# A hybrid encoder trunk on one core: S5 turns' tables, a norm's squares, and the gates' place in the scans

## The chip, the core and the metric

The kernel runs on one core of one Trainium2 chip. The metric is the device time of one execution in microseconds (us), median of three runs. Engines by the profile's names: PE is TensorE, PEld its weight loads, DVE is VectorE, ACT is ScalarE, POOL is GpSimd, SP is SyncE, which issues most DMAs.

## The reference, cut to what matters

Two layers on a sequence of 512 tokens with 1024 channels, in float32. Each layer is: RMS norm, one input projection, two mixers side by side, one output projection, residual add, RMS norm, an MLP with squared ReLU, residual add. Layer 0 mixes with RWKV-7 and Mamba-2, layer 1 with S5 (a diagonal complex state space) and mLSTM. The change is in what leads from layer 0's MLP into layer 1's mixers.

```python
def rmsnorm(x, w):
    y = x * rsqrt(mean(x * x, axis=-1) + EPS)
    return y * w

# S5, per direction: state x[t] = abar * x[t-1] + bbar @ u[t], abar = exp(dt * (ar + i*ai))
mag = exp(dt * ar)
abr, abi = mag * cos(dt * ai), mag * sin(dt * ai)

# mLSTM gates, per head and direction, chunkwise with a running maximum
log_i = i_pre + i_b
log_f = log_sigmoid(f_pre + f_b)
b = cumsum(log_f); m_t = max(max(b[t] - b[s] + log_i[s]), b + m)
```

## The kernel before, in words

**Layout.** Activations lie as eight tiles of 128 channels by 512 tokens. A product with a 128-column block of weights is a group of 24 matmuls of 512 columns: the weights are loaded in float32 (`wraw`), split into a high part on ACT (`whi`, L87) and a rest on DVE (`wlo`, L88; on POOL for eight columns of the mLSTM), and each of eight k-blocks takes three matmuls (L99 to L101 in `mm3`, L112 to L114 in `project`). `wraw`, `whi` and `wlo` have two buffers each, and the matmuls of these groups write to two PSUM banks (`mm`).

**Order.** A planner writes each engine's order at build time: it takes instructions by their order in the program as they become ready on its own clock, and the chip then runs each engine's list in that order. In stretches marked as scheduled by hand (layer 1 up to the heads) PE keeps the order of the program; the other engines are still the planner's. A pool's tile may be written when the tiles that lay at its place before have been read for the last time.

**Layer 0's MLP (`mlp`).** Four quarters of up and down groups: an up group's result goes through ACT (`hid`, L219; `act`, L221), POOL (L223) and DVE (L224); a down group's result is evacuated by DVE (`evac`, L251, two buffers) and added to the residual tile `x` by POOL (L253). In program order the groups are 10 up, 8 down, 8 up, 8 down, 8 up, 8 down, 6 up, 8 down. After each group `beside` takes one step of a generator, here `S5.params`, and lets that step's DVE instructions come no earlier than the group's own evacuation.

**The S5 tables (`S5.params`).** 61 steps. Steps 13 to 44 make the matrices of eight blocks of channel groups; steps 45 to 47 write them through DMAs on POOL's queue (L1544, L1547), beside down groups 2 to 4 of the third quarter. Step 48 makes the decay table `rc` (one ACT copy of 2048 columns, L1554, two POOL memsets) and starts the turns, unit complex numbers `z[i]`: `square` takes three DVE instructions and ends with `unit`, four more, which brings the length back to one. Steps 48 to 52 hold eight squares. Steps 53 to 60 double the tables `cos` and `sin` by complex products (`cmul`, six DVE instructions, scratch in the free half of `sin`); the four of the last doubling stand beside down groups 0 to 3 of the last quarter. Step 61 copies the negated sine (one ACT copy of 2048 columns, L1601).

**Layer 1's norm.** `split` makes high and low parts of the eight residual tiles (ACT L128, DVE L129). `rms_scale` squares them on ACT (L140), three buffers; POOL adds them up (L145), six adds; two matmuls with ones sum over channels (L148, L149); ACT takes the root (L160) and DVE the reciprocal `rstd` (L167). The pool `pre1` of these tiles (12 KB a partition) lies on the left side of memory, where the MLP's tiles lay before. The first two column groups of the projection need no `rstd` to start; the third needs a bank, which the first gives back only through L1608, with `rstd`.

**The scans.** `S5.scan` has 20 steps, five for each quarter of the channel groups: two with 16 small matmuls each (L1638) into two banks and three DVE instructions (L1640 to L1642), two with a pair of scans (L1645, L1647), one with the way back (L1650 to L1655). After each step PE gets four dense steps (12 matmuls of the projection). `Mlstm.gates` is a generator of 14 steps; the first two run before the scans. Of the other twelve, call them g3 to g14: g3 is a softplus on DVE, g4 a transpose on PE (L1132) and two cumulative sums, g5 to g8 running maxima, g9 four results of which the first is `li` (L1164), g10 to g13 each a transpose on PE (L1174), of `li` in g11, g14 four small DVE products (`diag`, L1180) and a matmul that sums them (L1182). `S5_STEPS[3]` says from which scan step on one gates step is taken after each scan step: 4, so that g14 follows scan step 15. `S5_STEPS[4]` is the number of dense steps behind each gates step that is left over after the scans; there is none before. Then seven dense steps, the outputs of S5 (L1680 to L1682) with the rest of the 128 dense steps, and the heads.

Of the kernel before, what the change touches and what calls it, by code (L numbers as in the profile page):

```python
# [13 lines left out]
AF = mybir.ActivationFunctionType  # L14
ALU = mybir.AluOpType
# [11 lines left out]
class Core:  # L27
# [102 lines left out]
                                           op0=ALU.mult, op1=ALU.subtract)  # L130
        return hi, lo

    def mean_square(self, xs):

        nc = self.nc
        n = xs[0].shape[1]
        acc = None
        for x in xs:
            sq = self.tile(self.io, [128, n], "sq", 3)
            nc.scalar.activation(sq, x, AF.Square)  # L140
            if acc is None:
                acc = sq
            elif x is not xs[-1]:
                nxt = self.tile(self.io, [128, n], "sqa", 2)
                nc.gpsimd.tensor_tensor(out=nxt, in0=acc, in1=sq, op=ALU.add)  # L145
                acc = nxt
        ps = self.aux()[:, 0:n]
        nc.tensor.matmul(ps, lhsT=self.ones, rhs=acc, start=True, stop=False)  # L148
        nc.tensor.matmul(ps, lhsT=self.ones, rhs=sq, start=False, stop=True)  # L149
        return ps  # L150

    def rms_scale(self, xs, pool, root=True, pieces=False):

        nc = self.nc
        ps = self.mean_square(xs)
        n = xs[0].shape[1]
        t = self.tile(self.io, [128, n], "ms", 1)
        r = self.tile(pool, [128, n], "rstd", 1)
        if root:
            nc.scalar.activation(t, ps, AF.Sqrt, bias=self.eps, scale=1.0 / 1024)  # L160
        else:
            nc.vector.tensor_scalar(out=t, in0=ps, scalar1=1.0 / 1024, scalar2=EPS,
                                    op0=ALU.mult, op1=ALU.add)
        if pieces:
            inverse(nc, r, t)
        else:
            nc.vector.reciprocal(out=r, in_=t)  # L167
        return r
# [98 lines left out]
PREP = (2, 3)  # L267
SPLIT = 6
END = (4, 24)
S5_STEPS = 8, 8, 4, 4, 3  # L270
OUT_STEPS = (0,) * 10 + (0, 1, 1) * 11 + (0,) * 8
NA = 2
DECAY = float(np.exp(-0.5))
# [1055 lines left out]
class S5:  # L1329
# [16 lines left out]
    def params(self, kp, tp):  # L1346

        c, nc = self.c, self.c.nc
# [5 lines left out]
        lent = [x.rearrange("p g c -> p (g c)") for x in (self.cos, self.sin[:, 0], self.sin[:, 1])]  # L1354
# [54 lines left out]
        x = tt(t("x"), dt, ar, M)  # L1409
# [35 lines left out]
        ts(pr[:, 1], am1, 1.0, Ad)  # L1445
        tt(pi[:, 1], mag, sin, M)

        def cmul(outr, outi, ar_, ai_, br_, bi_, shape, eng2=None):

            e2 = eng2 or V  # L1450
            self.n += 1
            names = ("a", "b", "c", "d")[:len(shape) - 1]
            cut = lambda x: x.rearrange(f"p ({' '.join(names)}) -> p {' '.join(names)}", **dict(zip(names, shape[1:])))
            t1, t2, t3, t4 = (cut(lent[2][:, 512 * i:512 * i + int(np.prod(shape[1:]))]) for i in range(4))
            V.tensor_tensor(out=t1, in0=ar_, in1=br_, op=M)
            e2.tensor_tensor(out=t2, in0=ai_, in1=bi_, op=M)
            V.tensor_tensor(out=outr, in0=t1, in1=t2, op=Sb)
            e2.tensor_tensor(out=t3, in0=ar_, in1=bi_, op=M)
            V.tensor_tensor(out=t4, in0=ai_, in1=br_, op=M)
            e2.tensor_tensor(out=outi, in0=t3, in1=t4, op=Ad)  # L1460
# [40 lines left out]
        for gb in range(8):  # L1501
            G = slice(4 * gb, 4 * gb + 4)
# [48 lines left out]
        r8 = tt(t("r8"), mag, mag, M)  # L1551
        tt(r8, r8, r8, M)
        tt(r8, r8, r8, M)
        nc.scalar.activation(self.rc, r8.unsqueeze(2).to_broadcast([128, 32, 64]), AF.Copy)  # L1554
        nc.gpsimd.memset(self.rc[0:64, :, 0:1], 0.0)
        nc.gpsimd.memset(self.rc[64:128, :, 63:64], 0.0)

# [9 lines left out]
        def unit(x):  # L1567
            tt(zq, x, x, M)
            tt(zq[:, 0], zq[:, 0], zq[:, 1], Ad)
            ts(zq[:, 0], zq[:, 0], -0.5, M, 1.5, Ad)  # L1570
            tt(x, x, zq[:, 0:1].to_broadcast([128, 2, 32]), M)

        def square(o, x, two=2.0):
            tt(zq, x, x, M)
            stt(o[:, 1], x[:, 0], two, x[:, 1], M, M)
            tt(o[:, 0], zq[:, 0], zq[:, 1], Sb)
            unit(o)

        unit(z[0])
        square(z[6], z[0])  # L1580
        yield
        square(z[0], z[6])
        square(z[1], z[0], sgn)
        yield
        for i in range(1, 6):
            square(z[i + 1], z[i])
            if i % 2:
                yield

        tr, ti = self.cos, self.sin[:, 0]  # L1590
# [2 lines left out]
        for i in range(6):  # L1593
            k = 1 << i
            n = min(32, 256 // k)
            for G in (slice(g, g + n) for g in range(0, 32, n)):
                b = lambda x: z[i + 1][:, x, G].unsqueeze(2).to_broadcast([128, n, k])
                cmul(tr[:, G, k:2 * k], ti[:, G, k:2 * k], tr[:, G, 0:k], ti[:, G, 0:k], b(0), b(1), (128, n, k))
                if k >= 4:
                    yield  # L1600
        nc.scalar.activation(self.sin[:, 1], ti, AF.Copy, scale=-1.0)  # L1601
        yield

    def columns(self, i, ps, rstd):
        c, nc = self.c, self.c.nc
# [151 lines left out]
def trunk(tc, ap, out):  # L1757
    nc = tc.nc
    with ExitStack() as ctx:
# [130 lines left out]
        with ExitStack() as left:  # L1890
# [8 lines left out]
            w_in = ap["cd_in"]  # L1899
            with ExitStack() as right:  # L1900
                xnp = right.enter_context(pool("xn1", "right"))
                with pool("pre1") as pre:
                    c.io = pre
                    xn = [c.split(x, xnp, 8, mix_w[1][:, k:k + 1]) for k, x in enumerate(X)]
                    rstd = c.rms_scale(X, io)
                c.io = io
                sa = right.enter_context(pool("s5_a", "right"))
                column = lambda i, use, eng=None: c.project(w_in[i], 128, xn, lambda ps: use(ps, rstd), eng)
# [107 lines left out]
```

## Time and profile before

| | us |
|---|---|
| three runs | 1800.29, 1802.35, 1804.42 |
| median | 1802.35 |
| the profiled execution | 1804.32 |
| its span, first to last instruction | 1802.5 |
| PE busy in it | 1697.4 |
| DVE, ACT, POOL busy | 1184.7, 733.7, 543.7 |

The profiled execution lies 1.97 us above the median, and its span 1.8 us below its own time. A row of the waits says which engine stood still, at which line, until which instruction ended. A row of the timeline gives start, duration, engine, line, operation, output and inputs, and in brackets how long the engine was idle before it. A row of busy time by stretch gives the stretch, its length, the busy time of each engine with its count of instructions, the granted TensorE clock as a share of 2.4 GHz, and the share and rate of the DMA engines.

### The profile page before, as it was taken

To read this page: it belongs to the slowest core of one execution; us is meant where nothing else is said; L and a number is where in the kernel's file an instruction comes from. 1 tells how busy PE (TensorE), PEld (TensorE's weight loads), DVE (VectorE), ACT (ScalarE), POOL (GpSimd) and SP (SyncE) were. 2 spreads that over 40 slices of the span, in tenths; PEclk is the share of its full clock that TensorE was granted. 3 is DMA by queue.
4 is the path that set the end of the run, shared out by engine and by line. 5 is a ranking of instruction groups with operands and counts; after the bars stand their busy time and mean duration, and the time that the engine had idled before them with its cause. 6 is when DMAs were issued, how large, how long until landed. Compare 5 with 4: busy or idle time off the path is not lost.

```text
span 1802.5 us, 26376 instructions
## 1 busy us (share of the span) xinstructions
PE 1697.4 (94%) x10124; PEld 1355.1 (75%) x10124; DVE 1184.7 (66%) x2110; ACT 733.7 (41%) x1263; POOL 543.7 (30%) x528
## 2 busy tenths in 40 slices
PE   7989999999899999999998989799799999999997
PEld 5777767678677877777786767587577688888887
DVE  6879796876777386657465849964658734353545
ACT  5635454433743343231322333335746432323243
POOL 4312131310452214666551323300221222222222
PEclk9999999899899999999998999889999999999999
DMA  4230202123402222433351366354321333323241
GB/s 166 80 94 19 66 25 80 29 71 117 143 13 80 75 93 75 136 101 122 129 173 60 101 204 167 122 184 108 89 87 53 100 93 94 94 94 105 94 132 67
DMA packets 90046, 177.40 MB, mean 98 GB/s; under 512 B 32688, under 2 KB 39600, under 8 KB 89792
## 3 DMA queue, kind: packets, MB, share of 16 engines
q1 hardware_dynamic: 82176, 157.32, 28.4%
q0 software_dynamic: 3200, 11.05, 1.8%
q10 hardware_dynamic: 4544, 7.34, 1.1%
q8 instruction: 80, 1.31, 0.3%
q14 instruction: 46, 0.38, 0.1%
HBM read 149.24 MB, written 28.54 MB: 99 GB/s over the span
## 4 chain that ended last, share of the span: by engine, by line
PE 38%; DVE 8%; ACT 3%; issue 3%; POOL 2%; DMA 0%; DVEq 0%; POOLq 0%; ACTq 0%
PE mm L99 10%; PE mm L100 9%; PE mm L101 9%; PE mm L112 1%; PE mm L113 1%; PE mm L114 1%; DVE wlo L88 1%; DVE s_w L1647 1%; PE mm L1272 1%; POOL hid L223 1%; POOL sqa L145 0%; DVE s_w L1642 0%; ACT whi L87 0%; DVE s_w L1645 0%; PE mm L1277 0%
## 5 line engine op out<-in xcount | busy, mean ns | idle before, releaser
L99 PE MATMUL mm<-act,whi 128*128 128x512 f32 (+1 forms) x1264 | 486.6, 386 | 12.1 <-ACT hid L219 3.1
L101 PE MATMUL mm<-act,wlo 128*128 128x512 f32 (+1 forms) x1264 | 483.9, 383 | 5.4 <-DVE wlo L88 5.0
L100 PE MATMUL mm<-act,whi 128*128 128x512 f32 (+1 forms) x1264 | 482.6, 382 | 0.6 <-DVE act L126 0.5
L87 ACT ACTIVATE whi<-wraw 128x1024 fp32r<-128x1024 f32 (+1 forms) x230 | 227.4, 989 | 581.2 <-PE mm L100 450.3
L88 DVE TENSOR_TENSOR wlo<-wraw,whi 128x1024 fp32r<-128x1024 f32 (+1 forms) x222 | 300.4, 1353 | 176.1 <-ACT whi L87 173.4
L99 PEld LDWEIGHTS mm<-act,whi 128*128 128x128 f32 x1264 | 239.2, 190 | 62.1 <-ACT hid L219 4.4
L101 PEld LDWEIGHTS mm<-act,wlo 128*128 128x128 f32 x1264 | 239.5, 190 | 56.8 <-DVE wlo L88 11.5
L100 PEld LDWEIGHTS mm<-act,whi 128*128 128x128 f32 x1264 | 239.7, 190 | 48.0 <-DVE act L126 1.4
L112 PE MATMUL mm<-act,whi 128*128 128x512 f32 (+1 forms) x464 | 205.3, 442 | 2.2 <-DVE pad L77 1.8
L114 PE MATMUL mm<-act,wlo 128*128 128x512 f32 (+1 forms) x464 | 188.2, 406 | 2.2 <-DVE wlo L88 2.2
L113 PE MATMUL mm<-act,whi 128*128 128x512 f32 (+1 forms) x464 | 186.7, 402 | 0.0
L223 POOL TENSOR_TENSOR hid<-hid 128x512 f32<-128x512 f32 x64 | 94.4, 1475 | 237.5 <-ACT hid L219 228.3
L253 POOL TENSOR_TENSOR x<-x,evac 128x512 f32<-128x512 f32 x56 | 83.8, 1497 | 184.0 <-DVE evac L251 176.1
L251 DVE TENSOR_TENSOR evac<-mm,rstd 128x512 f32<-128x512 f32 (+1 forms) x72 | 45.2, 628 | 108.0 <-PE mm L101 108.0
L112 PEld LDWEIGHTS mm<-act,whi 128*128 128x128 f32 (+1 forms) x464 | 89.4, 193 | 27.4 <-issue 4.5
L114 PEld LDWEIGHTS mm<-act,wlo 128*128 128x128 f32 (+1 forms) x464 | 89.3, 192 | 25.2 <-DVE wlo L88 3.1
L113 PEld LDWEIGHTS mm<-act,whi 128*128 128x128 f32 (+1 forms) x464 | 89.7, 193 | 15.6 <-issue 1.7
L224 DVE TENSOR_TENSOR act<-hid,act 128x512 fp32r<-128x512 f32 x64 | 45.0, 704 | 60.1 <-POOL hid L223 60.1
L145 POOL TENSOR_TENSOR sqa<-sqa,sq 128x512 f32<-128x512 f32 (+1 forms) x30 | 38.4, 1279 | 45.3 <-ACT sq L140 43.3
L76 POOL MEMSET pad<- 128x2 f32 x34 | 3.6, 111 | 152.8 <-DVE sh L768 55.3
L77 DVE TENSOR_TENSOR pad<-mm,rstd 128x512 f32<-128x512 f32 x32 | 21.9, 684 | 42.3 <-PE mm L114 42.3
L1753 DVE TENSOR_TENSOR x<-mm,x 128x512 f32<-128x512 f32 x32 | 22.1, 690 | 40.9 <-PE mm L101 40.9
(562 smaller groups left out, 2858.9 us busy)
## 6 DMA issues: line engine op xcount, KB each, us to landing
wraw<-mlp_w SPq DMA_DIRECT2D x130, 512.0 KB, 3.5
wraw<-ab_in SPq DMA_DIRECT2D x34, 512.0 KB, 3.7
wraw<-cd_in SPq DMA_DIRECT2D x21, 512.0 KB, 3.6
x<-x SPq DMA_DIRECT2D x16, 256.0 KB, 4.0
wraw<-ab_out_b SPq DMA_DIRECT2D x8, 512.0 KB, 3.6
s_cm<-s_sin POOLq DMA_DIRECT2D x8, 512.0 KB, 4.7
s_bm<-s_bt POOLq DMA_DIRECT2D x8, 512.0 KB, 4.6
s_m<-s_bm SPq DMA_DIRECT2D x8, 512.0 KB, 6.0
```

The lines of the kernel that those rows point to most:

```text
L87: nc.scalar.activation(hi[:, :cols], raw[:, :cols], AF.Copy)
L88: (eng or nc.vector).tensor_tensor(out=lo[:, :cols], in0=raw[:, :cols], in1=hi[:, :cols].bitcast(F32), op=ALU.subtract)
L99: nc.tensor.matmul(out, lhsT=wh, rhs=xh, start=start and k == 0, stop=False)
L100: nc.tensor.matmul(out, lhsT=wh, rhs=xl, start=False, stop=False)
L101: nc.tensor.matmul(out, lhsT=wl, rhs=xh, start=False, stop=stop and k == n - 1)
L112: nc.tensor.matmul(out, lhsT=wh, rhs=xh, start=k == 0, stop=False)
L113: nc.tensor.matmul(out, lhsT=wh, rhs=xl, start=False, stop=False)
L114: nc.tensor.matmul(out, lhsT=wl, rhs=xh, start=False, stop=k == len(xs) - 1)
L223: nc.gpsimd.tensor_tensor(out=sq, in0=h, in1=h, op=ALU.mult)
L224: last[0] = nc.vector.tensor_tensor(out=lo, in0=sq, in1=hi.bitcast(F32), op=ALU.subtract)
L251: last[0] = nc.vector.tensor_tensor(out=t, in0=ps, in1=r2[:, a:b], op=ALU.mult)
L253: (nc.vector if b - a < T else nc.gpsimd).tensor_tensor(out=x, in0=x, in1=t, op=ALU.add)
```

## The change

Three edits. `S5.params` writes `rc` in two copies with a step each, normalises only `z[0]` and `z[1]` instead of all nine turns, goes through the last doubling from the highest groups down with its scratch in 1024 instead of 2048 columns, and copies the negated sine in three pieces as groups are done; it still has 61 steps, and each of the doublings' steps stands one group later than before. Layer 1's norm squares into the tile that later holds the mean (`ms`) and one more, 4 KB instead of 12, and its pool moves to the right side, above the tiles of `split`. The gates start after scan step 11 instead of 4, so that g12 to g14 are left over and take three dense steps each behind them.

```diff
--- before.py
+++ after.py
@@ -130,11 +130,21 @@
                                            op0=ALU.mult, op1=ALU.subtract)
         return hi, lo
 
-    def mean_square(self, xs):
+    def mean_square(self, xs, lean=None):
 
         nc = self.nc
         n = xs[0].shape[1]
         acc = None
+        if lean is not None:
+            acc, last = lean, self.tile(self.io, [128, n], "sq", 1)
+            for i, x in enumerate(xs):
+                nc.scalar.activation(last if i else acc, x, AF.Square)
+                if 0 < i < len(xs) - 1:
+                    nc.gpsimd.tensor_tensor(out=acc, in0=acc, in1=last, op=ALU.add)
+            ps = self.aux()[:, 0:n]
+            nc.tensor.matmul(ps, lhsT=self.ones, rhs=acc, start=True, stop=False)
+            nc.tensor.matmul(ps, lhsT=self.ones, rhs=last, start=False, stop=True)
+            return ps
         for x in xs:
             sq = self.tile(self.io, [128, n], "sq", 3)
             nc.scalar.activation(sq, x, AF.Square)
@@ -149,12 +159,12 @@
         nc.tensor.matmul(ps, lhsT=self.ones, rhs=sq, start=False, stop=True)
         return ps
 
-    def rms_scale(self, xs, pool, root=True, pieces=False):
+    def rms_scale(self, xs, pool, root=True, pieces=False, lean=False):
 
         nc = self.nc
-        ps = self.mean_square(xs)
         n = xs[0].shape[1]
         t = self.tile(self.io, [128, n], "ms", 1)
+        ps = self.mean_square(xs, t if lean else None)
         r = self.tile(pool, [128, n], "rstd", 1)
         if root:
             nc.scalar.activation(t, ps, AF.Sqrt, bias=self.eps, scale=1.0 / 1024)
@@ -267,7 +277,7 @@
 PREP = (2, 3)
 SPLIT = 6
 END = (4, 24)
-S5_STEPS = 8, 8, 4, 4, 3
+S5_STEPS = 8, 8, 4, 11, 3
 OUT_STEPS = (0,) * 10 + (0, 1, 1) * 11 + (0,) * 8
 NA = 2
 DECAY = float(np.exp(-0.5))
@@ -1445,13 +1455,14 @@
         ts(pr[:, 1], am1, 1.0, Ad)
         tt(pi[:, 1], mag, sin, M)
 
-        def cmul(outr, outi, ar_, ai_, br_, bi_, shape, eng2=None):
+        def cmul(outr, outi, ar_, ai_, br_, bi_, shape, eng2=None, room=512):
 
             e2 = eng2 or V
             self.n += 1
             names = ("a", "b", "c", "d")[:len(shape) - 1]
             cut = lambda x: x.rearrange(f"p ({' '.join(names)}) -> p {' '.join(names)}", **dict(zip(names, shape[1:])))
-            t1, t2, t3, t4 = (cut(lent[2][:, 512 * i:512 * i + int(np.prod(shape[1:]))]) for i in range(4))
+            n = int(np.prod(shape[1:]))
+            t1, t2, t3, t4 = (cut(lent[2][:, room * i:room * i + n]) for i in range(4))
             V.tensor_tensor(out=t1, in0=ar_, in1=br_, op=M)
             e2.tensor_tensor(out=t2, in0=ai_, in1=bi_, op=M)
             V.tensor_tensor(out=outr, in0=t1, in1=t2, op=Sb)
@@ -1551,7 +1562,9 @@
         r8 = tt(t("r8"), mag, mag, M)
         tt(r8, r8, r8, M)
         tt(r8, r8, r8, M)
-        nc.scalar.activation(self.rc, r8.unsqueeze(2).to_broadcast([128, 32, 64]), AF.Copy)
+        for G in (slice(0, 16), slice(16, 32)):
+            nc.scalar.activation(self.rc[:, G], r8[:, G].unsqueeze(2).to_broadcast([128, 16, 64]), AF.Copy)
+            yield
         nc.gpsimd.memset(self.rc[0:64, :, 0:1], 0.0)
         nc.gpsimd.memset(self.rc[64:128, :, 63:64], 0.0)
 
@@ -1574,17 +1587,17 @@
             tt(zq, x, x, M)
             stt(o[:, 1], x[:, 0], two, x[:, 1], M, M)
             tt(o[:, 0], zq[:, 0], zq[:, 1], Sb)
-            unit(o)
 
         unit(z[0])
         square(z[6], z[0])
         yield
         square(z[0], z[6])
         square(z[1], z[0], sgn)
+        unit(z[1])
         yield
         for i in range(1, 6):
             square(z[i + 1], z[i])
-            if i % 2:
+            if i in (3, 5):
                 yield
 
         tr, ti = self.cos, self.sin[:, 0]
@@ -1593,13 +1606,16 @@
         for i in range(6):
             k = 1 << i
             n = min(32, 256 // k)
-            for G in (slice(g, g + n) for g in range(0, 32, n)):
+            for g in range(32 - n, -1, -n):
+                G = slice(g, g + n)
                 b = lambda x: z[i + 1][:, x, G].unsqueeze(2).to_broadcast([128, n, k])
-                cmul(tr[:, G, k:2 * k], ti[:, G, k:2 * k], tr[:, G, 0:k], ti[:, G, 0:k], b(0), b(1), (128, n, k))
+                cmul(tr[:, G, k:2 * k], ti[:, G, k:2 * k], tr[:, G, 0:k], ti[:, G, 0:k], b(0), b(1), (128, n, k), room=256)
+
+                G = G if g else slice(0, 16)
+                if k == 32 and g != 8:
+                    nc.scalar.activation(self.sin[:, 1, G], ti[:, G], AF.Copy, scale=-1.0)
                 if k >= 4:
                     yield
-        nc.scalar.activation(self.sin[:, 1], ti, AF.Copy, scale=-1.0)
-        yield
 
     def columns(self, i, ps, rstd):
         c, nc = self.c, self.c.nc
@@ -1899,10 +1915,10 @@
             w_in = ap["cd_in"]
             with ExitStack() as right:
                 xnp = right.enter_context(pool("xn1", "right"))
-                with pool("pre1") as pre:
+                with pool("pre1", "right") as pre:
                     c.io = pre
                     xn = [c.split(x, xnp, 8, mix_w[1][:, k:k + 1]) for k, x in enumerate(X)]
-                    rstd = c.rms_scale(X, io)
+                    rstd = c.rms_scale(X, io, lean=True)
                 c.io = io
                 sa = right.enter_context(pool("s5_a", "right"))
                 column = lambda i, use, eng=None: c.project(w_in[i], 128, xn, lambda ps: use(ps, rstd), eng)
```

## Rows read from the trace of the kernel before

**Rows 1.** waits of PE, 930 to 1200: total us, times, longest us

```profile
PE aux L1174 <- DVE ml_li L1164: 10.6, 1, 10.6
PE aux L148 <- POOL sqa L145: 5.3, 1, 5.3
PE mm L99 <- DVE s_zq L1376: 2.9, 1, 2.9
PE mm L99 <- ACT hid L219: 2.8, 2, 1.4
PE mm L99 <- DVE evac L251: 2.8, 1, 2.8
PE aux L1182 <- DVE ml_diag L1180: 2.4, 1, 2.4
```

**Rows 2.** busy time by stretch: length, engines, clock, DMA share, GB/s

```profile
950.00:960.00 10.00, 7.08 (x19) 5.33 (x18) 5.45 (x16) 1.06 (x1) 1.28 (x1) 0.66 0.24 84
...
980.00:990.00 10.00, 10.00 (x39) 8.06 (x38) 9.88 (x40) 2.18 (x3) 4.64 (x5) 0.83 0.14 50
...
1005.00:1045.00 40.00, 39.99 (x176) 32.73 (x176) 32.66 (x49) 14.07 (x17) 14.80 (x12) 1.00 0.34 107
```

**Rows 3.** timeline of DVE, 951 to 979

```profile
951.98 1.23 DVE L88 TENSOR_TENSOR wlo<-wraw,whi 128x1024 fp32r<-128x1024 f32 x1 [4.15 <-ACT whi L87]
953.12 0.69 DVE L251 TENSOR_TENSOR evac<-mm,rstd 128x512 f32<-128x512 f32 x1
...
978.83 0.68 DVE L251 TENSOR_TENSOR evac<-mm,rstd 128x512 f32<-128x512 f32 x1
```

**Rows 4.** groups of DVE instructions, 940 to 1026: busy us, mean ns of one

```profile
L1376 DVE TENSOR_TENSOR s_zq<-s_zq 128x32 f32<-128x32 f32 x9 | 2.5, 278 | 0.2
L1368 DVE TENSOR_SCALAR s_zq<-s_zq 128x32 f32<-128x32 f32 x9 | 2.5, 273 | 0.2
L1376 DVE TENSOR_TENSOR s_z<-s_z,s_zq 128x64 f32<-128x64 f32 x9 | 2.0, 223 | 0.2
```

**Rows 5.** timeline of ACT, POOL, PE and DVE at the norm

```profile
1042.54 0.40 PE L112 MATMUL mm<-act,whi 128*128 128x512 f32 x1
...
1044.84 0.72 ACT L128 ACTIVATE act<-x,c_norms 128x512 fp32r<-128x512 f32 x1 [1.27 <-POOL pad L76]
1045.47 1.66 ACT L140 ACTIVATE sq<-x 128x512 f32<-128x512 f32 x3
...
1048.06 6.69 POOL L145 TENSOR_TENSOR sqa<-sqa,sq 128x512 f32<-128x512 f32 x5
...
1054.81 2.08 PE L148 MATMUL aux<-sqa,ones 128*128 128x512 f32 x2 [5.35 <-POOL sqa L145]
...
1059.35 3.35 DVE L167 RECIPROCAL rstd<-ms 128x512 f32<-128x512 f32 x1 [3.51 <-ACT ms L160]
```

**Rows 6.** timeline of POOL and DVE running at once, last quarter

```profile
1011.18 4.22 POOL L253 TENSOR_TENSOR x<-x,evac 128x512 f32<-128x512 f32 x1 [3.44 <-DVE evac L251]
...
1011.36 0.41 DVE L1456 TENSOR_TENSOR s_sin<-s_sin,s_z 128x256 f32<-128x256 f32 x1
...
1016.55 1.52 DVE L1456 TENSOR_TENSOR s_sin<-s_sin,s_z 128x256 f32<-128x256 f32 x1
```

**Rows 7.** scans from 1121.5 by stretch: all engines, then DVE on tile s_w alone

```profile
1121.50:1194.00 72.50, 59.48 (x263) 47.66 (x262) 71.19 (x86) 23.89 (x33) 25.52 (x14) 0.84 0.37 126
...
1121.50:1194.00 72.50, 46.12 (x37) 0.84 0.37 126
```

**Rows 8.** timeline of PE: small scan matmuls, and the wait for li

```profile
1136.01 1.89 PE L1638 MATMUL mix<-s_ul,s_m 128*128 128x64 f32 x16
...
1154.74 0.69 PE L1174 MATMUL aux<-ident,ml_li 64*128 64x64 f32 x4 [10.62 <-DVE ml_li L1164]
```

**Rows 9.** groups of DVE instructions, 1093 to 1194: the two results behind li

```profile
L1165 DVE SCALAR_TENSOR_TENSOR ml_lf<-ml_b,ml_cm 64x512 f32<-64x512 f32 x1 | 2.8, 2844 | 0.0
...
L1166 DVE TENSOR_TENSOR ml_x<-ml_g,ml_small 64x512 f32<-64x512 f32 x1 | 1.8, 1759 | 0.0
```

## What the change was forecast to do

> **What bounds the kernel.** I read the waits of PE first, for the part of the run that the change touches, because an edit to DVE, ACT or POOL shows in the time only where PE stands still for it. Between 930 and 1200 us six waits matter [rows 1]. Three (2.9, 2.8 in two pieces, 2.8) lie at the end of layer 0's MLP, one of 5.3 at layer 1's norm, two of 10.6 and 2.4 in the scans. Then the stretches: beside the last quarter of the MLP, 1005 to 1045, PE is busy 39.99 of 40 us with 176 matmuls, 0.227 us each [rows 2], so there PE is the bound; in the scans DVE is, busy 71.19 of 72.5 us while PE is busy 59.48 [rows 7]. A wait also costs what comes after it: after the first, 950 to 960, the granted clock is 0.66, after the third, 980 to 990, it is 0.83 [rows 2]; that is part of the stretch at the lower of the two levels, 1.2 GHz.
>
> **Edit 1, the tables.** Of nine normalisations two stay. One is four dependent DVE instructions; three have rows, 0.278, 0.273 and 0.223, and the first is taken as the second: 1.05 us. Seven fewer take 7.3 us off DVE [rows 4]. Does PE wait for them? The second wait, in two pieces, ends with ACT's reading of a bank, `hid`, and the third with an evacuation. The first names a turn's product, `s_zq`, but PE reads nothing of that; the evacuation just before it frees the bank. The timeline of DVE shows why: evacuations come only at 953.12 and 978.83, the first right behind a weight split that waited 4.15 us for ACT [rows 3]. That is an order written by the planner; the evacuations of the seventh and eighth down group were late on its clock. The turns' instructions come behind these evacuations, and the next turns after 953.12 are over before the split that holds the last one. What could make an evacuation late is its buffer, which POOL's add gives back, and POOL has the matrices' DMAs in its list there (steps 45 to 47). The change doesn't touch those. So I expect the same order and the same three waits, and take **0** for the edit; after 980 DVE is full (9.88 of 10) but PE does not stand still. The later steps are covered as well: one more product step falls behind the fifth down group of the last quarter; six instructions at about 0.41, 2.5 us [rows 6], and 1005 to 1045 has 7.3 us of DVE free [rows 2]. The copies of `rc` and of the sine stay on ACT, busy 14.07 of 40 there, and their users come 40 us or more later. Two more ACT copies and no DMA are issued. Ends: the three waits go, with what their slow clock cost, or they come a second time. The waits are 8.5. The clock: 950 to 960 has 7.1 us outside the wait and 19 matmuls where 31 fit at 0.227, 2.7 us lost; 980 to 990 has 39 where 44 fit, 1.1 lost. Together 12.3, so the ends are -12.3 and +12.3.
>
> **Edit 2, the norm.** Now the squares begin only at 1045.47, behind the split of the last `x` (to 1045.56), although seven of the eight tiles were final long before; their memory is the MLP's until then. Five of POOL's six adds fill 1048.06 to 1054.75, and PE, which has the ones matmul early in its order, waits 5.35 us and runs it slowly, 2.08 for two passes [rows 5]. In free memory each square needs only its `x`. One pair of tiles makes the chain serial, but a new `x` comes only once per group of 24 matmuls, 24 x 0.227 = 5.4 us, and a square and an add take about 0.55 + 1.34 (1.66 / 3 and 6.69 / 5 [rows 5]), 1.9 us. So after the last split only one square is left, done at 1046.2, and the matmuls can run inside the first two column groups. The root and the reciprocal (3.35 [rows 5]) then end near 1052. PE had reached 1049.5 when it began to wait; the 18 matmuls left of the second column and the two sums, at full clock some 2 us, take it to 1055.6, so the third column finds a bank free. What goes: the wait, 5.3, and half of the ones matmuls' 4 us (the second pair taken like the first), 1.9. What comes: the planner may put the second ones matmul into PE's list before 1046.2. The first column begins at 1042.54 [rows 5], so that wait lies between 0 and 3.7; I take 1.2, as the planner's clock was ahead of the chip's by the whole 5.35 us over six adds before, and only one square and one add are left. Sum **-6.0**, ends -7.2 and -3.5. On SP the first S5 matrix load now lies on the norm's 4 KB and must wait for the reciprocal; the loads of weights queued behind it have two buffers ahead, and the scans need it 40 us later: 0.
>
> **Edit 3, the gates.** DVE is full in the scans, so moving gates steps frees nothing by itself; what counts is when `li` (g9) is done against when PE comes to g11. Before, PE came at 1144.1 (1154.74 less 10.62 [rows 8]). The prefix up to scan step 12 is the same. Behind it now stand seven sets of 12 matmuls, 84 x 0.227 = 19.1, two sets of small ones at 1.89 [rows 8] and short transposes: PE arrives at about 1167. DVE ends the first quarter at 1121.5 either way. Of its 71.2 us after that, 46.1 are scan work on `s_w`, another 4.1 are the six L1641 (the same shape as the evacuation's 0.68 [rows 3]), 2.4 two weight splits (1.23 each [rows 3]); 18 remain for g4 to g14. Of these 2.8 and 1.8 [rows 9] and some 1.7 of short ones lie behind `li`, so 12 lie up to it. If DVE keeps program order, `li` comes after two quarters (33.5), half of the last (8), 12 and 2.4: 1177.4, a wait of 10.4 where it was 10.6. The wait for `diag` in g14 can be 1 to 7 where it was 2.4. I take **0**: the clock's losses after two waits stay about as they are. Ends: nothing waits but `diag` early, -8; everything of the gates behind the scans, worked out below, +6.
>
> **Sum.** 0 - 6.0 + 0 on the profiled execution's 1804.32 gives 1798.3. That execution lies 1.97 above the median of the runs shown, so the median of the changed kernel is forecast at 1802.35 - 6.0 = **1796.3**.
>
> **A page against the trace.** In the last quarter a DVE product beside POOL's add took 1.52 where it otherwise takes 0.41, and a POOL add beside a run of products took 4.22 [rows 6]. The Trainium skill, SBUF — State Buffer, "Who interferes with whom", says that a DVE instruction with two SBUF inputs and a GpSimd instruction that reads SBUF exclude each other for a whole instruction. The trace agrees with it. It speaks against this change, which carries six POOL adds from an empty stretch into one full of such products; the third rival is what that would do here.
>
> **Rivals.** First, *the MLP's waits go too*: with lighter steps the planner finds the two evacuations ready in time. For it: DVE's list there is what changes most. Against it: what holds them seems to be POOL. It gives -6.0 - 12.3: 1784.0. Second, *the scans take the gain back*: the planner puts all of g4 to g9 behind the last quarter, so `li` comes at 1121.5 + 50.2 + 12 + 2.4 = 1186, a wait of 19, and `diag` none more: +6 against 13.0 before, 1802.3. For it: the gates' steps now come last in the program; against: an instruction that is ready and comes before others is taken in turn, as the interleaving before shows. Third, *slower*: POOL's queue in the last quarter. POOL is busy 14.8 of 40 us there [rows 2]; six adds at up to 4.22 would bring it to 40. If an add stands ahead of the `x` add of a group and holds it back longer than a group, 5.4 us, the second evacuation behind it finds no buffer, a bank stays taken, and PE waits as it does now from 951 to 980: +12.3, so 1808.6. Below 5.4 us the two banks cover it. Against it: on average POOL has room. That the change doesn't do what it says, the squares still coming after the MLP, would show as a norm wait longer than now, as one buffer makes a chain of 1.9 us a piece; it ends like the third, and is counted with it.
>
> **Chances.** Forecast 0.52, its own range 1790 to 1800; first rival 0.15; second 0.15; third 0.18. The range leaves out the third and takes in the other cases: 1782 to 1806. Runs of this kernel differ enough that 0.2%, 3.6 us, is about what can be told from no change. Faster by more than that means under 1798.7: the forecast but for 0.03 of it, and the first rival, 0.64. Within it lie the second rival and that 0.03: 0.18. Slower: 0.18.
>
> **What would show it.** Right: no wait at L148 over 2 us, squares from about 1010 on, the third column begun before 1060; evacuations near 953 and 979 still late; one wait of 8 to 12 at L1174 and a short one at L1182, some 20 us later than now. Wrong: PE without waits from 951 to 980, or waits for evacuations between 1005 and 1045, or a wait at L1174 above 15.

## The result, and the profile after

The changed kernel takes 1812.09 us (median of 4) where the kernel before, run beside it, takes 1802.92: a ratio of 1.0054, 95% interval 1.0037 to 1.0072. That is 9.2 us slower; forecast was 1796.3, range 1782 to 1806. Its profiled execution took 1813.02, span 1811.2.

The waits of PE in the changed kernel, 930 to 1250 us: total us, times, longest.

```profile
PE mix L1237 <- ACT ml_ch L1178: 13.1, 1, 13.1
PE mix L1238 <- DVE ml_cl L1179: 6.8, 1, 6.8
PE mm L99 <- DVE evac L261: 5.7, 2, 2.9
PE mm L114 <- DVE wlo L88: 5.3, 2, 3.3
PE mix L1654 <- DMA s_ul<-s_ud: 4.7, 1, 4.7
PE aux L145 <- POOL ms L143: 3.3, 1, 3.3
PE mm L99 <- ACT hid L229: 2.8, 2, 1.4
PE mm L101 <- DVE wlo L88: 1.5, 3, 1.1
```

Against [rows 1]: the MLP's waits are all still there (5.7 and 2.8). The norm's 5.3 has become 3.3. The wait for the scans' input `s_ul` has grown from 1.5 to 4.7, those for weight splits from 0.5 in all to 5.3 and 1.5. New are 13.1 and 6.8 for `ml_ch` and `ml_cl`, the negated running maximum of the gates in two parts, where 10.6 and 2.4 stood before for `li` and `diag`.

**Where the input comes from.** The timeline of SP (which issues DMAs), kernel before, from the last two columns of S5 to the scans:

```profile
1071.10 0.32 SPq L1609 DMA_DIRECT2D s_ud<-sh  x1
1072.23 0.33 SPq L86 DMA_DIRECT2D wraw<-cd_in  x1
1076.68 0.32 SPq L1609 DMA_DIRECT2D s_ud<-sh  x1
1077.82 0.33 SPq L86 DMA_DIRECT2D wraw<-cd_in  x1
1078.73 11.99 SPq L1624 DMA_DIRECT2D s_ul<-s_ud  x8
1094.75 1.29 SPq L86 DMA_DIRECT2D wraw<-cd_in  x2
```

The same of the changed kernel:

```profile
1064.37 0.32 SPq L1625 DMA_DIRECT2D s_ud<-sh  x1
1065.51 0.33 SPq L86 DMA_DIRECT2D wraw<-cd_in  x1
1065.89 0.45 SPq L1631 DMA_DIRECT2D s_m<-s_bm  x1
1069.93 0.32 SPq L1625 DMA_DIRECT2D s_ud<-sh  x1
1070.34 0.89 SPq L1631 DMA_DIRECT2D s_m<-s_bm  x2
1072.02 16.16 SPq L1640 DMA_DIRECT2D s_ul<-s_ud  x8
1088.28 1.63 SPq L86 DMA_DIRECT2D wraw<-cd_in  x2
```

The fourth column is written out 6.8 us earlier (1069.93 against 1076.68), but the input's eight issues now take 16.16 us instead of 11.99. Two S5 matrices of 512 KB are loaded right ahead of them, and the weight load that went ahead of them before stands behind. The timeline of PE shows what follows, kernel before and then the changed kernel; in brackets the idle time before an instruction:

```profile
1094.31 2.00 PE L1638 MATMUL mix<-s_ul,s_m 128*128 128x64 f32 x16 [1.53 <-DMA s_ul<-s_ud]
```

```profile
1091.20 3.41 PE L1654 MATMUL mix<-s_ul,s_m 128*128 128x64 f32 x16 [4.74 <-DMA s_ul<-s_ud]
...
1098.91 0.79 PE L114 MATMUL mm<-act,wlo 128*128 128x512 f32 x1 [3.34 <-DVE wlo L88]
```

Between the first and the second set of small matmuls lie 12.1 us where 6.2 lay before (1094.31 to 1100.55); the first set takes 3.41 instead of 2.00, and the granted clock from 1091 to 1104 is 0.52 where it was 0.87.

**The last quarter of the MLP.** The timeline of DVE, changed kernel, a tables' step under one of POOL's new adds, and PE's wait behind it:

```profile
1012.15 1.51 DVE L1467 TENSOR_TENSOR s_sin<-s_sin,s_z 128x256 f32<-128x256 f32 x1
1013.58 0.41 DVE L1469 TENSOR_TENSOR s_sin<-s_cos,s_z 128x256 f32<-128x256 f32 x1
1013.92 0.41 DVE L1468 TENSOR_TENSOR s_cos<-s_sin 128x256 f32<-128x256 f32 x1
1014.25 1.51 DVE L1470 TENSOR_TENSOR s_sin<-s_sin,s_z 128x256 f32<-128x256 f32 x1
1015.68 1.21 DVE L88 TENSOR_TENSOR wlo<-wraw,whi 128x1024 fp32r<-128x1024 f32 x1
```

```profile
1016.95 0.50 PE L101 MATMUL mm<-act,wlo 128*128 128x512 f32 x1 [1.05 <-DVE wlo L88]
```

A step's six products before held at most one of 1.5 us [rows 6]; here there are two or three, and the split behind them comes late.

**Two marks to count from.** Executions differ by up to 9 us ahead of some 980 us, where PE has the same list in every kernel here, so places are counted from the end of the MLP's last wait. That is 979.57 before and 975.32 after. The first transposes of the gates, which follow the four columns, start at 1086.53 and 1079.77: 106.96 and 104.45 after the mark, so 2.5 us are gained. The second set of small matmuls starts 120.98 and 128.02 after it, 7.0 lost. The heads' first transposes of results (1272.28 and 1279.85) come 292.71 and 304.53 after it, 11.8 lost. So of the loss 9.5 us arise between the columns' end and the second set, and 4.8 later. All runs in this way, us against the kernel before's profile:

| | columns done | first set | second set | heads | ratio to before | 95% interval |
|---|---|---|---|---|---|---|
| changed kernel | -2.5 | +1.1 | +7.0 | +11.8 | 1.0054 | 1.0037, 1.0072 |
| t_only | -1.1 | -0.9 | -2.5 | -2.2 | 0.9989 | 0.9976, 1.0002 |
| n_only | -2.9 | +0.7 | +4.5 | +4.1 | 1.0027 | 1.0011, 1.0043 |
| g_only | 0.0 | 0.0 | 0.0 | +5.2 | 1.0012 | 0.9999, 1.0025 |
| tn | -2.5 | +1.2 | +6.5 | +5.3 | 1.0019 | 1.0005, 1.0032 |
| n_skip | -6.4 | -3.2 | +1.2 | +1.2 | 1.0013 | 1.0002, 1.0024 |
| n_ul_pool | -3.1 | +1.1 | +2.8 | +4.3 | 1.0007 | 0.9998, 1.0016 |
| n_m6 | -3.6 | -3.7 | -5.3 | -4.3 | 0.9978 | 0.9968, 0.9988 |
| before_m6 | +0.1 | -0.2 | -1.8 | +0.1 | 0.9994 | 0.9983, 1.0005 |
| tn_dve | -4.1 | -0.5 | +4.8 | +4.7 | 1.0027 | 1.0014, 1.0039 |
| tn_dve_m6 | -4.1 | -4.3 | -5.9 | -2.0 | 0.9982 | 0.9966, 0.9997 |
| tn_m6 | -3.3 | -2.8 | -2.9 | -4.4 | 0.9978 | 0.9966, 0.9989 |
| after_m6 | -3.2 | -2.5 | -2.5 | +1.9 | 1.0001 | 0.9988, 1.0014 |
| g_neg_pool | -0.2 | -0.2 | -0.2 | +5.2 | 1.0033 | 1.0021, 1.0045 |
| g_all_pool | -0.1 | -0.3 | -0.3 | +5.0 | 1.0041 | 1.0027, 1.0055 |
| t_start8 | +0.1 | +0.2 | -1.3 | +3.4 | 1.0013 | 1.0000, 1.0026 |
| tn_m6_split | -3.6 | -3.2 | -3.3 | -2.0 | 1.0019 | 1.0008, 1.0029 |

The places come from one execution each; kernels with the same code up to a place differ there by up to about 1 us. The ratios come from all runs taken beside the kernel before and are not always the quotient of the two medians. Where places and ratio disagree the ratio decides.

### The profile page after: what moved, and what is told of

It is laid out like the page before. It is cut to its first block, busy times and chain, and to the rows that moved or that the text cites. A ratio compares the mean times of both kernels' runs of the same rounds, so it can differ in the third digit from the quotient of the medians.

```text
span 1811.2 us, 26347 instructions
## 1 busy us (share of the span) xinstructions
PE 1689.9 (93%) x10124; PEld 1348.9 (74%) x10124; DVE 1189.1 (66%) x2082; ACT 736.1 (41%) x1267; POOL 544.2 (30%) x528
## 5 line engine op out<-in xcount | busy, mean ns | idle before, releaser
L99 PE MATMUL mm<-act,whi 128*128 128x512 f32 (+1 forms) x1264 | 485.7, 385 | 11.8 <-DVE evac L261 5.7
L155 POOL TENSOR_TENSOR sqa<-sqa,sq 128x512 f32<-128x512 f32 (+1 forms) x25 | 31.7, 1268 | 45.2 <-ACT sq L150 43.6
```

Of the source, the lines that this page charges most:

```text
L99: nc.tensor.matmul(out, lhsT=wh, rhs=xh, start=start and k == 0, stop=False)
```

## Experiments

### The three edits apart

Each of three kernels makes one edit alone; the fourth is the changed kernel with the gates' start undone:

```diff
-S5_STEPS = 8, 8, 4, 11, 3
+S5_STEPS = 8, 8, 4, 4, 3
```

> The tables' edit alone, norm and gates as before. Theory A (the loss comes from the norm's edit, through the order of the loads on SP's queue before the scans, and from the gates' edit, through ACT's list): the tables lie beside PE's work, the waits of 2.8 to 2.9 us near 953 and 976 stay, the time lies between 4 us below and 2 above before. Rival B (the lighter steps move DVE's list so that a weight split comes late in the last quarter of the MLP, as the 1.05 us wait at 1017 of the changed kernel hints): 3 us or more above before.

> The norm's edit alone, tables and gates as before. Theory A: the wait of 5.3 us at the ones matmul shrinks to some 3, but the loads of the scans' input, eight on SP's queue, now stand ahead of a weight load that stood ahead of them before; PE waits some 4.7 us for that input and 3.3 for the weight split behind it, and the time is 0 to 5 us above before. Rival C (the norm keeps its gain, and the gates' edit alone makes the loss): 5 to 6 us below before.

> The gates' start alone, 11 in place of 4. Theory A: PE waits 13 us for the copy of the running maxima on ACT and some 7 for its rest on DVE, in place of 10.6 and 2.4 for the gates' transposes: 4 to 7 us above before. Rival C: the gates make the whole loss and the norm's gain as well, 12 to 15 above before. Rival D (the gates' place costs nothing, as forecast): within 2 us of before.

> The changed kernel with the gates' start put back to 4. Theory A: the sum of the first two, between 3 us below and 5 above before, so 4 to 7 below the changed kernel. Rival C: 5 to 6 below before, some 15 below the changed kernel.

Tables alone: 1800.25 against 1803.4, not to be told from no change, and the MLP's waits stay (5.7 and 2.8). Norm alone: 1808.28, 4.9 us above before, with waits of 4.7 for the input and 1.6 for the split behind it. Gates alone: 1805.81, 2.4 above, its interval just taking in no change. Tables and norm together: 1806.09, some 6 us below the changed kernel by the ratios (1.0019 against 1.0054). The norm's edit loses by itself, so rival C falls; the tables' does not, so B falls. The gates' 2.4 is under the 4 to 7 of theory A and at the edge of rival D's 2; its place at the heads is +5.2, and the last group of runs measures it again. The lists of the kernels agree: the changed SP order comes with the norm's edit and in no other, and the list that puts `ml_ch` ahead in the scans comes with the gates' start alone.

### Why the norm's edit loses

> The norm's edit alone, without POOL's first three adds of squares (the sum leaves out three of the eight channel tiles). Theory A (POOL's adds stretch the tables' products on DVE in the last quarter, so weight splits come late): no wait for a split at 1022 and 1028 us, one product in six at 1.5 us as before instead of three, and 1 to 2 us less up to the norm. Rival (the splits are late because ACT's squares stand ahead of the high parts): the waits of 1.0 and 0.2 us stay, since the squares are all still there.

```diff
-                if 0 < i < len(xs) - 1:
+                if 3 < i < len(xs) - 1:
                     nc.gpsimd.tensor_tensor(out=acc, in0=acc, in1=last, op=ALU.add)
```

One product of DVE in n_only, then the same in n_skip, 1005 to 1030 us (busy us, mean ns):

```profile
L1469 DVE TENSOR_TENSOR s_sin<-s_sin,s_z 128x256 f32<-128x256 f32 x4 | 3.9, 964 | 0.0
```

```profile
L1469 DVE TENSOR_TENSOR s_sin<-s_sin,s_z 128x256 f32<-128x256 f32 x4 | 1.6, 410 | 0.0
```

Without the three adds the waits for splits at the MLP's end are back at the 0.5 of the kernel before (1.8 in n_only), and the columns are done 3.5 us earlier (-6.4 against -2.9). Waits make 1.6 of that, 1.3 for splits and 0.3 at the norm's sums; the rest is not traced. The squares on ACT are the same in both, so the rival falls. The input still comes late (4.3 us of wait), and by the second set the gain is spent.

> The norm's edit alone, with the eight loads of the scans' input on POOL's queue instead of SP's; SP then has the weight loads right behind the S5 matrices. Theory A (the norm's gain is lost because two weight loads stand behind the eight input loads on SP's queue): no wait for a weight split between the first and the second set of small scan matmuls, these 6 to 7 us apart as before instead of 9 to 12, and a time 3 to 6 us below that of the norm's edit alone, so at or under before. Rival (the input itself comes late because its own transfers do, whatever queue they stand in): the wait for the input grows by what the splits' wait loses, and the time stays where the norm's edit alone has it, some 5 us above before.

```diff
-            nc.sync.dma_start(ul[16 * j:16 * j + 16], us[j])
+            nc.gpsimd.dma_start(ul[16 * j:16 * j + 16], us[j])
```

A half each. The split's wait between the sets is gone and the sets lie 8.0 us apart instead of 10.0, so the weight load behind the input on SP did cost; 6 to 7 were expected, and a split's wait of 3.5 appears at 1188 instead. The wait for the input is 5.3, as the rival has it: on another queue it is as late. The time, 1803.38 against 1802.32, has a lower ratio than n_only, but the intervals overlap. What else stands beside the input are the matrices:

> The norm's edit alone, with six buffers instead of eight for the S5 matrices, so that two of the eight loads of 512 KB can't go ahead of the scans' input, and on SP's queue a weight load stands ahead of the input's eight loads again. Theory A2 (without the norm's wait, the matrices' loads that used to fill it run together with the scans' input, which comes some 3.5 us later after the fourth column than before): the wait for the input falls from 4.7 to between 1 and 3 us, no split is waited for over 1 us before the second set of small matmuls, that set begins 3 to 6 us earlier than in the norm's edit alone counted from the MLP's end, and the time is 3 to 5 us below it if the outputs don't wait for their matrices. Rival (the input's transfers take their time whatever else is loaded): the wait stays at 4 us or more.

```diff
-            bm = self.c.tile(kp, [128, 4, 2, 128], "s5_m", 8)
+            bm = self.c.tile(kp, [128, 4, 2, 128], "s5_m", 6)
...
-                mats.append([c.tile(kp, [128, 8, 128], "s5_m", 8) for _ in range(3)])
+                mats.append([c.tile(kp, [128, 8, 128], "s5_m", 6) for _ in range(3)])
```

The timeline of SP in n_m6, for the fences above:

```profile
1068.69 0.32 SPq L1619 DMA_DIRECT2D s_ud<-sh  x1
1069.82 0.33 SPq L86 DMA_DIRECT2D wraw<-cd_in  x1
1070.86 11.70 SPq L1634 DMA_DIRECT2D s_ul<-s_ud  x8
```

The input is issued in 11.70 us, PE waits 0.9 for it, and the kernel takes 1798.36 where before takes 1802.76. That is 4.4 us faster, and some 9 below n_only by the ratios, which differs from it by two buffers. Expected were 3 to 5: the theory had the direction and half of the size. The second set alone comes 9.8 us earlier (-5.3 against +4.5), 4.4 of it before the first set and 5.4 between the two. The control asks whether six buffers alone do that:

> The kernel before with six buffers for the S5 matrices instead of eight, nothing else. Theory A2 (before, the matrices' loads found room in the norm's wait, so they cost the scans' input little): the wait for the input stays between 0 and 1.5 us and the time is within 2 us of before. Rival (six buffers are a gain by themselves, here or in the outputs): 4 to 6 us below before.

1802.53 against 1802.85: no difference, and a wait for the input of 1.3. So eight buffers cost time only beside the norm's edit. Before, PE stood from 1049.5 to 1054.8 and ran the sums slowly to 1058.6 [rows 5], and SP had the first six matrices issued by 1057.2 and all eight by 1067.4; the first column was written out only at 1063.93. In the changed kernel two matrices go out at 1044.31, then SP stands 8.5 us until the first column is written out at 1053.65, and the other six stand behind that in its list, the last two at 1070.34, with the input. That the planner orders them so because the columns come earlier is the likely reading; but the prediction also has the norm's tiles lying where the first matrix goes, and no run separates the two. The six buffers change two things at once, the loads ahead of the input and the weight load's place. In n_ul_pool, where no weight load waits behind the input, the input is as late, so the second alone does not seem to make it late; that kernel also changes the queue.

### Adds on DVE

> Tables and norm as changed, gates as before, with the six adds of squares on DVE instead of POOL. Theory B2 (a POOL add beside the tables' products costs DVE more than the add itself, two to three products at 1.5 instead of 0.41 us against 0.69 for an add on DVE): no wait for a split in the last quarter of the MLP, the wait at the first ones matmul under 2 us instead of 3.2, and 1 to 4 us below tables and norm with POOL's adds. Rival (DVE is the fuller engine there, so its adds delay splits and evacuations): waits for splits of over 1.5 us in all, and no gain.

> Both of these together, tables and norm as changed, gates as before. If both theories hold it is 4 to 9 us below tables and norm alone, so 1 to 6 us below before; if the rivals hold it stays 1 to 5 us above before.

```diff
-                    nc.gpsimd.tensor_tensor(out=acc, in0=acc, in1=last, op=ALU.add)
+                    nc.vector.tensor_tensor(out=acc, in0=acc, in1=last, op=ALU.add)
```

Waits for splits in the last quarter shrink from 1.5 to 0.6, but the first ones matmul waits 2.9 where it waited 3.2, and the time is 1807.61 against 1802.76: no gain over POOL's adds (a ratio of 1.0027 against 1.0019). With six buffers it is 1799.51, no better than with POOL's (below). The columns are done 0.8 to 1.6 us earlier with DVE's adds, which the time doesn't show. Theory B2's gain falls; of its rival the missing gain holds, the delayed splits don't.

### The gates

> The gates' start at 11 alone, with the negated maxima copied by POOL instead of ACT, and the heads' mask made only after the gates, so that no matmul of the heads can be drawn ahead into the scans. Theory E (the two waits of 13.4 and 6.8 us come from ACT's list, held by that copy, and from the drawn matmuls): both go, PE runs on and waits under 10 us in all for the gates' transposes, and the time falls 4 us or more below the gates' edit alone. Theory F (DVE's list makes them: it holds the first weight split behind the gates' steps and the last quarter of the scans): PE waits about as long, 18 to 22 us in all, but for that split, and the time is within 2 us of the gates' edit alone.

```diff
-        nc.scalar.activation(self.ch, cm, AF.Copy, scale=-1.0)
+        nc.gpsimd.tensor_scalar(out=self.ch, in0=cm, scalar1=-1.0, scalar2=None, op0=ALU.mult)
...
+        nc.vector.tensor_scalar(out=late, in0=self.dec[:, 0, 0:1], scalar1=0.0, scalar2=1.0, op0=ALU.mult, op1=ALU.add)
+        nc.scalar.activation(self.neg, cst[:, 0:256].rearrange("p (d t) -> p d t", d=2), AF.Copy, scale=late[:, 0:1])
```

(The second part stands behind the last gates step; the mask `neg` was copied at the gates' start, without `late`, a number that is always one.) The timeline of PE, its only wait in the scans for anything but the input:

```profile
1183.21 0.79 PE L114 MATMUL mm<-act,wlo 128*128 128x512 f32 x1 [24.03 <-DVE wlo L88]
```

Both named waits are gone, and one of 24.0 stands in their place; 1808.11 is no faster than g_only. Theory E falls, and with it a reading of the waits by name: `ml_ch` was only the first of several things that came late together. Theory F named the split. The next kernel takes that out too:

> The gates' start at 11 alone, with the copy of the negated maxima on POOL, the heads' mask after the gates, and now also the first two weight splits that DVE holds behind the gates' steps on POOL. Theory F (PE stands still because DVE's list holds that split): the wait of 24.0 us for a split goes, PE waits 8 to 14 us in all up to the outputs, for the gates' transposes, and the time is 3 to 8 us below the version with the split on DVE, so -3 to +2 against before. Rival (late gates make PE wait whatever it has in its list): 18 us or more of waits in all, and the time stays 4 to 6 above before.

```diff
-ml.values(i, ps, r)) for i in range(8)]
+ml.values(i, ps, r), nc.gpsimd if i in (3, 4) else None) for i in range(8)]
```

The waits of PE in g_all_pool that take their place:

```profile
PE aux L1173 <- DVE ml_li L1163: 9.9, 1, 9.9
PE aux L1181 <- ACT ml_tok L1174: 5.5, 1, 5.5
...
PE aux L1173 <- DVE ml_g L1138: 2.2, 1, 2.2
PE aux L1173 <- ACT ml_tok L1174: 1.8, 1, 1.8
```

Together 19.4, and the time, 1808.95 against 1802.39, has not fallen. By the waits the rival holds: in all three lists that were tried PE waits 19 to 24 us for what comes behind the gates' steps. Theory F falls as far as it blames that split. The time says less, since the two splits on POOL cost some 7 us by themselves in tn_m6_split below, and no run takes the split out of DVE's list without that price.

What the three lists share is DVE. Its first sum of the gates and `li`, kernel before and then g_only:

```profile
1126.29 1.71 DVE L1136 TENSOR_TENSOR_SCAN ml_b<-c_ml_const,ml_lf 32x512 f32<-32x512 f32 x1
...
1154.00 0.68 DVE L1164 TENSOR_TENSOR ml_li<-ml_small,ml_cm 64x512 f32<-64x512 f32 x1
```

```profile
1158.53 2.31 DVE L1136 TENSOR_TENSOR_SCAN ml_b<-c_ml_const,ml_lf 32x512 f32<-32x512 f32 x1
...
1174.93 0.68 DVE L1164 TENSOR_TENSOR ml_li<-ml_small,ml_cm 64x512 f32<-64x512 f32 x1
```

The gates' sums start some 32 us later, behind nearly two more quarters of the scans, and `li` comes some 21 us later, inside the last quarter. DVE has no room to make that up: it is busy 70.91 of the 72.5 us from 1121.5 in the changed kernel, as before [rows 7], while PE's busy time there falls from 59.48 to 50.66. No run takes work off DVE there without putting it on POOL, so this reading is argued from the traces and not shown.

> The tables' edit with the gates' start at 8, between 4 and 11. Theory F (PE's loss is DVE's full list; what matters is that PE has dense work to do that needs no split from DVE while the gates' steps run): the waits for the gates' transposes shrink from 14.7 us in all to 5 to 10, the first weight split on DVE stands ahead of the last quarter's scans and is not waited for over 3 us, and the time is 2 to 6 us below the tables' edit alone. Rival (later gates cost more, step by step): 1 to 3 us above it.

1803.81 against 1802.32, a higher ratio than the tables alone, though the intervals meet: waits of 8.4, 3.4, 2.2, 1.8 and 1.5 make 17. The rival again, later gates cost more; F's forecast of a gain was wrong.

### What remains of the change, and a version that beats both

> The changed kernel with six buffers for the S5 matrices. Theories A2 and F together (the loads make some 7 to 9 us of the changed kernel's loss, the gates' start the rest): 6 to 10 us below the changed kernel, so -1 to +4 against before, with the input's wait under 2 us and PE's waits at the gates still 18 to 24 us in all. Rival (the gates' place makes nearly all of it): 0 to 3 below the changed kernel.

> Tables and norm as changed with POOL's adds, six buffers, gates' start at 4 as before. If the parts add up (tables -2, norm with six buffers -4.4): 4 to 9 us below before, the fastest of all. If the tables' edit gives nothing beside it: 2 to 5 below.

> Tables and norm as changed, six buffers, gates' start at 4, and the same two weight splits on POOL. Theory F: with early gates DVE's list holds no split that PE waits for in the scans (the waits there are for the gates' own results), so 2.4 us less on a full DVE is all: 0 to 3 us below the version with these splits on DVE. Rival (POOL's two splits, each beside DVE's products, stretch those by as much): 0 to 2 above it.

The changed kernel with six buffers is level with before (1802.73 against 1802.85), 9.4 us below the changed kernel. With the gates' start undone as well it takes 1798.87, 4.0 below before; that and n_m6 are the fastest, and the tables' edit adds nothing to the second. Along this path the loss of 9.2 splits into -4.0 for tables and norm, 3.9 for the gates' start (1802.73 - 1798.87) and 9.4 for the loads' place. By other pairs the gates' start costs 2.4 (g_only) to 6 (the changed kernel against tn) and the loads' place 7 (tn against tn_m6, by the ratios); the order of the two sizes is the same. Waits of PE in tn_m6:

```profile
PE aux L1184 <- DVE ml_li L1174: 10.6, 1, 10.6
...
PE aux L145 <- POOL ms L143: 3.3, 1, 3.3
...
PE mix L1654 <- DMA s_ul<-s_ud: 1.5, 1, 1.5
```

Two weight splits on POOL lose 7 us on it (1806.21 against 1802.39). The direction is the rival's, the size more than any theory had; the place of the heads shows 2.4 of it and the rest is open.

## Why the forecast was wrong, step by step

- **Edit 1, 0.** Held. The three MLP waits stayed with their sizes, though the row now names `evac` for the wait that named `s_zq` before: as the prediction read it, the product was not what PE waited for. The first rival fell with that.
- **Edit 2, the norm itself.** The wait at the first ones matmul was worked out as 0 to 3.7, taken as 1.2; it is 2.1 in n_only and 3.3 in the changed kernel. The third column began at 1057.36, before 1060 as said. From the mark that is less: 82.0 us after it, where 1060 on the clock of the kernel before is 80.4. The gain by the columns' end is 2.5 to 3.6 where 6 was forecast, and n_skip, with half the adds, has 6.4. The missing part comes from the cause that the third rival started from, POOL's adds among DVE's products, at 3.5 us instead of 12.3, but not by its path: no `x` add held back an evacuation; DVE's products grew longer and weight splits came late. The prediction saw the 1.52 us product and looked only at what POOL's queue would hold back; the sum charged DVE nothing. One product in n_skip takes 410 ns where it takes 964 in n_only. The rule that the prediction took from the Trainium skill (SBUF — State Buffer, "Who interferes with whom") agrees with that; it should have gone into the sum.
- **Edit 2, SP.** This is the step that failed: "the loads of weights queued behind it have two buffers ahead, and the scans need it 40 us later: 0". The loads were priced by their own users. Left out was what stands behind them: the scans' input, which PE needs soon, is issued last, after the fourth column. Before, all eight matrices were issued 9 us ahead of that column's write-out; with the edit two of them stand right ahead of the input, and a weight load behind it. PE waits 4.7 for the input and 3.3 for a weight split behind it, so the two buffers did not cover the queued weights either. Price: 9.4 us (after_m6 against the changed kernel; 7 to 9 by the other pairs). Nor did the first matrices wait for the reciprocal: two were issued at 1044.31, and it ran from 1048.99.
- **Edit 3, 0.** The place of `li` was read rightly, inside the last quarter: 1177.4 forecast, PE there at 1167 and a wait of 10.4. In g_all_pool, whose list of PE is as the prediction assumed, PE waits 9.9 until 1177.65. That the times agree so well is luck: counted from the mark, PE's arrival and the wait's end both come some 4 us later than forecast. What was mis-sized is what stands around it: 2.2 for `ml_g` and 1.8 and 5.5 for what follows `li`, where 2.4 was taken, so 19.4 in all against 13.0 before. In the changed kernel the planner drew the heads' matmuls L1237 and L1238 into the scans, which the prediction didn't foresee, but that isn't the cost: without them the loss is as large. 3.9 us lies inside the ends given, -8 to +6.
- **The second rival** (the scans take the gain back, at the gates) had the nearest size there, a wait of 19 where the two waits make 19.9, but not the mechanism: `li` did not come behind the last quarter. It had no part in the larger loss.
- **The signs.** Squares from 1009.93 and late evacuations came as said, the wait at the ones matmul (3.3) and the one at `li` did not. None of the signs of being wrong appeared. They looked at the waits that the three edits touch, and the larger loss lies at another, for the scans' input.

## What to carry to other kernels

A stall on one engine is free time for another: before removing it, list what the queues did in it, and ask where those transfers go next and what they will stand beside. A wait's named releaser can be the last of several late things; if taking it away only changes the name, look for what they all stand behind. Price an added instruction by what it does to its neighbours on the shared path, not only by its own engine's idle time.

## What the runs showed of the hardware that was not expected

The scans' input, eight transfers of 128 KB, is issued by SP in 11.26 to 12.36 us in the kernels with no matrix load right ahead, and in 14.96 to 16.16 in those with two. The waits of SP from 1070 to 1100 us say where the time went, kernel before and then the changed kernel:

```profile
SPq L1624 <- DMA ml_xm<-pad: 4.8, 1, 4.8
...
SPq L1624 <- DMA wraw<-cd_in: 1.9, 1, 1.9
```

```profile
SPq L1640 <- DMA ml_xm<-pad: 4.7, 1, 4.7
...
SPq L1640 <- DMA s_m<-s_bm: 4.3, 1, 4.3
...
SPq L1640 <- DMA ml_xc<-sh: 2.2, 1, 2.2
```

An issue of the input waits for a matrix load to land, which it doesn't read, and for the mLSTM's stores from ACT's queue. The semaphores in the trace's records say why: the DMAs of SP and ACT all count on the same eight semaphores, POOL's on eight others, and each of these waits ends within 0.03 us of the landing of the last transfer that used the issue's own one (the second matrix landed at 1077.71, and the issue that took over its semaphore began at 1077.72). So it is the way this program counts its transfers that holds the issue, and no limit of the chip is shown by it.

It is not the whole of the lateness. In n_ul_pool, where POOL's own semaphores had long been free, all eight are issued by 1081.54, yet the last lands at 1090.95, and PE starts 21.8 us after the issue of the fourth column's write-out: 21.2 in n_only, 21.3 in the changed kernel, 17.6 before and 17.4 in n_m6. There the input shares the time with two matrices and with weight loads that no longer queue behind it. How much of the changed kernel's wait comes from the semaphores and how much from transfers that run at the same time, no run separates.
